# The first head of the second half of a retention and convolution decoder layer: two projection quads run in turn, both in seven block products

## The chip, the cores and the metric

The kernel runs on one core of one Trainium2 chip. The metric is the time of one execution on the device in microseconds (us), taken as the median over runs. TensorE is called PE here, VectorE DVE, ScalarE ACT, GpSimd POOL, and SyncE, whose queue issues nearly all transfers, SP.

## What is computed

```python
def mixer_layer(h, norm_g, w_in, conv_w, ret_norm_g, w_out, pos):
    hn = rms_norm(h, norm_g)
    proj = jnp.einsum('bld,de->ble', hn, w_in)                 # 1024 -> 8 * 512
    cx, cb, cc, cg, q, k, v, rg = jnp.split(proj, N_PROJ, axis=-1)
    conv_out = short_conv_branch(cx, cb, cc, conv_w) * jax.nn.silu(cg)
    qf = rotary(q.reshape(shp), pos) * (RET_HEAD_DIM ** -0.5)  # 4 heads of 128
    kf = rotary(k.reshape(shp), pos)
    ret = head_group_norm(retention_chunkwise(qf, kf, vf), ret_norm_g)
    mixed = jnp.concatenate([conv_out, ret * jax.nn.silu(rg)], axis=-1)
    return h + jnp.einsum('ble,ed->bld', mixed, w_out)
```

16 meta tokens stand ahead of a sequence of 2048, all in float32; a last RMS norm follows.

## The kernel before

The sequence is worked in two rounds (`r`) of 1024 columns, each round in two column blocks of 512 (`j`). In a round come eight units: four retention heads and four convolution groups. In round 0 the order ends with convolution group 3, and round 1 begins with head 0. Each unit needs two **quads**. A quad is a product of four weight blocks (K or Q and V or gate, against two halves of the model dimension) with the four blocks of x (two halves by two column blocks). Keys and values are the first quad of a head, queries and gates the second.

To keep the accuracy of float32, every operand is split in a high and a low part (`mh`, `ml` of x, `wh`, `wl` of a weight): ACT casts the high part, DVE subtracts it to get the low part (`split`, lines 116 to 125). A block product over four slices of 128 is three matmuls per slice, 12 in all, each 128 by 128 against 512 columns.

There are two ways to run a quad. `quad` (line 241) does it in **seven** block products, by sums of blocks in the manner of Strassen and Winograd: 84 matmuls. Its operands are x blocks 0, 1, 5 and four sums of x blocks (slots 2, 3, 4, 6 of `operand`), and seven weight blocks, which go through a ring of three buffers (`wh`, `wl`, `RING = 3`). Products 0, 2, 4 and 6 accumulate in one PSUM bank, 1 in a second, 3 and 5 in a third. After product 0, 2 and 3 ACT copies the bank (line 259), after 1, 4, 5 and 6 the `take` of the unit adds the copy on DVE and goes on. `quad_plain` (line 298) does the quad in **eight** products, from the plain blocks: 96 matmuls.

The sums of x for round 1 are made during round 0 and stored (`sums_x`). Round 1's first head uses `quad_plain` for keys and values, from 16 loads of x (`moving`) and four weights that are kept whole in operand slot 3 (`plain_parts`). Two of the four sums are loaded and split behind that, the other two by `rest_of_sums` after the first quad, together with the late gating of convolution group 3 (`gate_late`, lines 722 to 728: four DVE multiplies, two activations on ACT, two POOL multiplies). Then `quad` does queries and gates.

Keys and queries go through `rotary` (lines 738 to 745: four DVE instructions, of which the first two work on 64 partitions each). Values and keys are turned by a transposing DMA (`part`, `cross`).

Every engine runs its instructions in the order in which a list scheduler put them when the program was built; it moves instructions within what the data allow. `tc.issue_after(ins)` gives it one more rule of order. Semaphores make an engine wait for a value that another one has not yet made; what stands behind the waiting instruction on that engine waits too.

Of the kernel before, what the change touches and what calls it, by code (L numbers as in the profile page):

```python
# [8 lines left out]
F32 = mybir.dt.float32  # L9
# [69 lines left out]
def hybrid_trunk(ctx: ExitStack, tc: tile.TileContext, t, out: bass.AP, chunk_decay):  # L79
# [102 lines left out]
    def moving(load, scale=None, after={}, behind={}):  # L182
# [11 lines left out]
                    after.get((j, k), lambda: None)()  # L194
        return m, blocks

    def block_sums(b11, b12, b22, b21, t1, t3, f, g):

        def less(out, a, factor, b):
            if factor is None:
                sub(nc.vector, out, a, b)
            else:
                nc.vector.scalar_tensor_tensor(out=out, in0=a, scalar=factor, in1=b, op0=ALU.mult, op1=ALU.subtract)  # L205

        if f is not None:
# [15 lines left out]

    loaded = [None]

    def prepared(m, src, ns, held={}):

        for n in ns:
            for kt in range(KH):
                a = held.get((n, kt))  # L230
                if a is None:
                    a = gen("t")[:, :HB]
                    loaded[0] = nc.sync.dma_start(a, src[n, kt])
                parts(m, SUMS[n], kt, a)

    def idle():
# [4 lines left out]
    def quad(w, m, take, steps=()):  # L241


        steps = iter(steps)

        def product(i, bank, first):
            (wh, wl) = w[i]
            for kt in range(KH):
                ks = slice(kt * P, (kt + 1) * P)
                mh, ml = m[i][kt]  # L250
                for n, (a, b) in enumerate(((wl, mh), (wh, ml), (wh, mh))):
                    nc.tensor.matmul(  # L252
                        bank, a[:, ks], b, start=first and kt == 0 and n == 0, stop=kt == KH - 1 and n == 2,
                        skip_group_check=not first,
                    )
# [24 lines left out]
        product(4, xb, False)  # L280
        take(1, 1, xb, c)
        product(5, zb, False)
        take(0, 1, zb, u2)
        product(6, xb, False)
        take(1, 0, xb, None)

    def plain_part(n, load, slot):
        a = sb.tile([P, HB], F32, name="ra", tag="ra", bufs=RAW)
# [175 lines left out]
    def load_x(r):  # L464
        def load(k, j):
            a = gen("x")[:, :HB]
            if r == 0:
# [82 lines left out]
    def w_loads(n, r=0):  # L550
# [4 lines left out]
        return [lambda a, b=b: nc.sync.dma_start(a, b) for b in blocks]  # L555

    def kept_sums(n, r):
        return sums_a[n] if r == 0 and n in KEPT else None

    mixed = [  # L560
        dram.tile([2, 2, 2, P, KH, P], F32, name=f"mixed{b}", tag=f"mixed{b}") for b in range(SEQ // HB)
# [196 lines left out]
    def part(a, to_cross=None):  # L758
# [3 lines left out]
        if to_cross is None:  # L762
            cross(across, apart)
        else:
            to_cross.append((across, apart))
        return across

    waiting = [[], []]
# [13 lines left out]
    def head(h, r, m, rot_t, f, turning, blocks, ahead, sums, first=(), between=((), idle, idle, idle)):  # L782
# [1 line left out]

        to_cross, queried = [], []
# [5 lines left out]
        def take(i, j, pp, c):  # L793
            if i == 1 and c is None:
                v[j] = part(pp, to_cross if len(first) else None)
                return
            d = gen("kv")[:, :HB]
            if c is None:
                nc.scalar.copy(out=d, in_=pp)
            else:  # L800
                add(nc.vector, d, pp, c)
            if i == 0:
                rotary(d, tables[j])
                k[j] = d
            else:
                v[j] = d
                late.append(j)

        if len(first) > 0:
            quad_plain(first[0], m, take)  # L810
        else:
            with tc.issue_after(spreading[0].ins) if r + h == 0 else nullcontext():
                w = stationary(blocks[0], nc.vector if r + h == 0 else nc.gpsimd, kept_sums(2 * h, r))
            quad(w, m, take, between[0] or (finish_late,))
            catch_up(0)
        between[1]()
        if to_cross:
            with tc.issue_after(loaded[0].ins):
                for pair in to_cross:
                    cross(*pair)  # L820
        q, sg = [None, None], [None, None]

        def take(i, j, pp, c):
            d = gen("qg")[:, :HB]
            if i == 0:
                if c is None:
                    nc.scalar.copy(out=d, in_=pp)
                else:
                    add(nc.vector, d, pp, c)
                rotary(d, tables[j])  # L830
# [18 lines left out]
        def split_late():  # L849
            for j in late:  # L850
                v[j] = part(v[j])
            split_keys(0)

        def join(j):
# [15 lines left out]
            join_keys(0)  # L870
            between[3]()

        quad(stationary(load_raw(w_loads(2 * h + 1, r)), keep=kept_sums(2 * h + 1, r)), m, take, (split_late, middle, late_middle))
        with tc.issue_after(copied[0].ins):
            join(1)
            weigh(1)
            join_keys(1)
        between[2]()
        with tc.issue_after(queried[0].ins):
            next(sums, None)  # L880
# [191 lines left out]
    for r in range(NR):  # L1072
# [7 lines left out]
        if r == 0:  # L1080
# [70 lines left out]
                            parts(m, i, kt, held[kt])  # L1151

            between = (), idle, idle, idle
            later = prepare(load_x(1), sums_x, gain_of)
        else:
            m, b = moving(load_x(r), gain_of)
            first = [plain_parts(w_loads(0))]
            load_tables()
            prepared(m, sums_x, (1, 3))

            def rest_of_sums():
                with queued((lowered[0],)):
                    store_kept = kept.pop()()
                prepared(m, sums_x, (0, 2))
                with tc.issue_after(loaded[0].ins):
                    store_kept()

            between = (), rest_of_sums, idle, idle
# [74 lines left out]
```

## Time and profile before

| what | us |
|---|---|
| median of 3 runs | 866.44 (866.12 to 867.37) |
| the profiled execution, its own time | 865.16 |
| its span in the trace | 863.4 |
| PE busy | 854.4 (99% of the span) |
| DVE busy | 678.4 (79%) |
| ACT busy | 500.5 (58%) |
| POOL busy | 279.6 (32%) |

The page of the profile gives busy time by engine, groups of instructions by source line, and the chain of work that ended last. Durations of one instruction overlap with the next one's: what an instruction costs its engine in a row of equal ones is the distance from start to start, and it is read from rows in which several are merged. The profiled execution is 1.28 us below the median.

### The profile page before, as it was taken

The page shows a single profiled execution, that of the slowest core. Times are in us where ns is not written, and L with a number is a line of the kernel's source. Part 1 is how long each engine was busy: PE and PEld are TensorE (multiplying, and loading weights), DVE is VectorE, ACT ScalarE, POOL GpSimd, SP SyncE. Part 2 cuts the span into 40 slices and gives each one's busy share as a digit, 9 for nine tenths or more (in the row PEclk, how much of TensorE's full clock was granted, in tenths as well). Part 3 has the DMA queues.
Part 4 walks back from the last instruction along what each step waited for, and adds up shares of the span by engine and source line. Part 5 has one row for each costly group of instructions (what it writes and reads, how often), then busy time and mean ns, then how long its engine had stood idle before and what let it go on. Part 6 is the DMA issues. An engine that isn't in the chain of part 4 may idle for free.

```text
span 863.4 us, 12846 instructions
## 1 busy us (share of the span) xinstructions
PE 854.4 (99%) x4216; PEld 705.7 (82%) x4216; DVE 678.4 (79%) x1206; ACT 500.5 (58%) x901; POOL 279.6 (32%) x224
## 2 busy tenths in 40 slices
PE   9999999999999999999999999999999999999996
PEld 6778888878887778888888888888888878888885
DVE  6798989889897977979677787976655699766653
ACT  8775648474855654948284757544433575555553
POOL 0022332422245554110000002341312153777773
PEclk9999999999999999999999999999999999999999
DMA  8736257565777744966275667557344684555431
GB/s 320 244 127 167 91 147 215 146 190 184 183 232 244 244 147 159 341 195 171 74 186 170 167 189 177 174 135 256 101 118 122 201 323 147 159 177 178 147 134 74
DMA packets 141187, 154.43 MB, mean 179 GB/s; under 512 B 59904, under 2 KB 77632, under 8 KB 141120
## 3 DMA queue, kind: packets, MB, share of 16 engines
q1 hardware_dynamic: 140544, 153.21, 58.0%
q8 instruction: 33, 0.54, 0.3%
q10 hardware_dynamic: 576, 0.40, 0.2%
q14 instruction: 34, 0.28, 0.1%
HBM read 101.14 MB, written 39.85 MB: 163 GB/s over the span
## 4 chain that ended last, share of the span: by engine, by line
PE 95%; DVE 2%; DMA 1%; ACT 1%; issue 1%; POOLq 0%; SPq 0%; DVEq 0%
PE pj L252 76%; PE pj L333 5%; PE pj L309 5%; PE ms L919 2%; PE ms L908 2%; PE ms L918 2%; PE ms L895 2%; PE ms L506 1%; DMA w<-in_w_out 1%; PE ms L1057 1%; DVE wl L120 0%; DVE qg L948 0%; DVE x L205 0%; PE ms L381 0%; DVE u L663 0%
## 5 line engine op out<-in xcount | busy, mean ns | idle before, releaser
L252 PE MATMUL pj<-mh,wl 128*128 128x512 f32 x1008 | 395.8, 393 | 0.8 <-DVE wl L120 0.4
L252 PE MATMUL pj<-mh,wh 128*128 128x512 f32 x1008 | 393.2, 390 | 0.0
L252 PE MATMUL pj<-ml,wh 128*128 128x512 f32 x1008 | 392.7, 390 | 0.0
L119 ACT CAST wh<-ra 128x512 fp32r<-128x512 f32 x229 | 142.2, 621 | 253.5 <-PE pj L252 217.0
L120 DVE TENSOR_TENSOR wl<-ra,wh 128x512 fp32r<-128x512 f32 x229 | 189.1, 827 | 63.4 <-ACT wh L119 61.9
L252 PEld LDWEIGHTS pj<-mh,wl 128*128 128x128 f32 x1008 | 189.3, 188 | 41.8 <-ACT tc L259 1.2
L252 PEld LDWEIGHTS pj<-mh,wh 128*128 128x128 f32 x1008 | 189.2, 188 | 39.3
L252 PEld LDWEIGHTS pj<-ml,wh 128*128 128x128 f32 x1008 | 189.3, 188 | 38.3
L131 POOL TENSOR_TENSOR ra<-ra 128x512 f32<-128x512 f32 x44 | 67.7, 1540 | 80.6 <-PE ms L506 38.5
L931 POOL TENSOR_TENSOR rp<-rs,neg_half 128x4 f32<-128x4 f32 x16 | 19.2, 1202 | 149.8 <-DVE rs L128 149.6
L259 ACT COPY tc<-pj 128x512 f32<-128x512 f32 x108 | 62.8, 581 | 0.1
L128 POOL TENSOR_TENSOR sa<-ra 128x512 f32<-128x512 f32 x22 | 32.5, 1478 | 57.7 <-DMA ra<-in_w_in 46.6
L131 POOL TENSOR_TENSOR ra<-sa,ra 128x512 f32<-128x512 f32 x22 | 30.7, 1396 | 30.1 <-DVE wl L120 20.9
L994 DVE TENSOR_TENSOR yo<-pj,yo 128x512 f32<-128x512 f32 (+1 forms) x33 | 21.9, 672 | 23.1 <-PE pj L252 15.4
L1005 POOL TENSOR_TENSOR z<-yo,final_g 128x512 f32<-128x512 f32 x16 | 26.5, 1654 | 20.0 <-DVE yo L994 20.0
L935 DVE TENSOR_SCALAR pm<-ms,mv,rp 128x128 f32<-128x128 f32 x64 | 21.8, 403 | 11.0 <-POOL rp L931 11.0
L128 POOL TENSOR_TENSOR yo<-yo,tc 128x512 f32<-128x512 f32 x18 | 27.4, 1527 | 5.9 <-ACT tc L259 5.8
L663 POOL TENSOR_TENSOR c<-c,tc 128x512 f32<-128x512 f32 x12 | 18.6, 1551 | 31.8 <-ACT tc L693 28.4
L128 DVE TENSOR_TENSOR tc<-pj,tc 128x512 f32<-128x512 f32 x26 | 17.8, 684 | 14.1 <-PE pj L252 14.1
L663 POOL TENSOR_TENSOR c<-c,rr 128x512 f32<-128x512 f32 x12 | 18.8, 1563 | 27.1 <-DVE c L713 17.0
L581 DVE SCALAR_TENSOR_TENSOR c<-u,conv_w,c 128x512 f32<-128x512 f32 x32 | 25.2, 830 | 2.3 <-POOL u L572 1.2
L123 DVE SCALAR_TENSOR_TENSOR ml<-x,gain,mh 128x512 fp32r<-128x512 f32 x32 | 22.7, 746 | 5.1 <-ACT mh L122 5.0
(166 smaller groups left out, 1215.9 us busy)
## 6 DMA issues: line engine op xcount, KB each, us to landing
ra<-in_w_in SPq DMA_DIRECT2D x111, 256.0 KB, 2.9
ra<-sums_a SPq DMA_DIRECT2D x52, 256.0 KB, 2.9
x<-in_xT SPq DMA_DIRECT2D x48, 256.0 KB, 4.9
sums_a<-ra SPq DMA_DIRECT2D x42, 256.0 KB, 2.1
w<-in_w_out SPq DMA_DIRECT2D x32, 256.0 KB, 5.3
ra<-mixed SPq DMA_DIRECT2D x32, 256.0 KB, 2.6
yo<-in_x SPq DMA_DIRECT2D x32, 256.0 KB, 4.5
ra<-in_x SPq DMA_DIRECT2D x16, 256.0 KB, 3.3
```

The lines of the kernel that those rows point to most:

```text
L119: nc.scalar.copy(out=hi, in_=src)
L120: lowered[0] = eng.tensor_tensor(out=lo, in0=src, in1=hi.bitcast(F32), op=ALU.subtract)
L123: nc.vector.scalar_tensor_tensor(out=lo, in0=src, scalar=scale, in1=hi.bitcast(F32), op0=ALU.mult, op1=ALU.subtract)
L128: eng.tensor_tensor(out=out, in0=a, in1=b, op=ALU.add)
L131: eng.tensor_tensor(out=out, in0=a, in1=b, op=ALU.subtract)
L252: nc.tensor.matmul(bank, a[:, ks], b, start=first and kt == 0 and n == 0, stop=kt == KH - 1 and n == 2, skip_group_check=not first,)
L259: copied[0] = nc.scalar.copy(out=c, in_=bank)
L309: nc.tensor.matmul(banks[i], a[:, ks], b, start=half + kt + n == 0, stop=half == 1 and kt == KH - 1 and n == 2,)
L333: nc.tensor.matmul(banks[n][i], a[:, ks], b, start=half + kt + s == 0, stop=half == 1 and kt == KH - 1 and s == 2,)
L581: nc.vector.scalar_tensor_tensor(out=c, in0=u[:, tap : tap + HB], scalar=conv_w[:, g, tap : tap + 1], in1=c, op0=ALU.mult, op1=ALU.add)
L663: eng.tensor_tensor(out=out, in0=a, in1=b, op=ALU.mult)
L1005: nc.gpsimd.tensor_tensor(out=ys[i][j], in0=y, in1=final_g[:, j * HB : (j + 1) * HB], op=ALU.mult)
```

## The change

Round 1's first head runs both of its quads together, each in seven products. `quads` takes product 0 of keys and values, then product 0 of queries and gates, then product 1 of both, and so on to product 6; the four `pj` banks of PSUM hold both quads. I call product i of the first quad Pia and that of the second Pib. The 14 weight blocks come one by one through the same ring of three, each split right behind the products of the pair in front (`weights_in_turn`). Loads are issued in one line in the order of use: x blocks of product 0, two weights, x blocks of product 1, two weights, the sums of products 2 and 3, and so on; the second column block of the first half of x (slot 7) is not loaded any more. The late gating of convolution group 3 is put behind the splits of the last sum (`close_sums`, T4). The function `take` of a head becomes `take_keys` and `take_queries`, with one more rule of order for the first rotaries (`early`).

```diff
+    def moving_in_turn(load, scale, sums, ws):
+        m = [[] for _ in range(8)]
+        def blocks(half, j, kts=range(KH)):
+            for kt in kts:
+                k = half * KH + kt
+                parts(m, BLOCK[half][j], kt, load(k, j), scale(k) if scale else None)
+        blocks(0, 0)
+        leading = [next(a) for a in ws]
+        blocks(1, 0, range(KH // 2))
+        with tc.issue_after(copied[0].ins):
+            blocks(1, 0, range(KH // 2, KH))
+        steps = [
+            lambda: sums(m, 1), lambda: sums(m, 0), lambda: sums(m, 2), lambda: blocks(1, 1), lambda: sums(m, 3),
+        ]
+        return m, leading, steps
...
+    def quads(ws, w, m, takes, between=()):
...
+        for i in range(7):
+            for n in range(len(ws)):
+                if i < 2:
+                    banks[n][i] = ps_proj()
+                product(n, i, banks[n][i in (1, 3, 5)], i in (0, 1, 3))
+            w = [next(a, None) for a in ws]
+            for n, take in enumerate(takes):
+                bank = banks[n][i in (1, 3, 5)]
+                if i == 0:
+                    copies[n] = copy(bank)
+                elif i == 1:
+                    take(0, 0, bank, copies[n])
...
+                else:
+                    take(1, 0, bank, None)
+            next(between, idle)()
...
+    def weights_in_turn(n, r):
+        for load in w_loads(n, r, in_line):
+            a = raw()
+            load(a)
+            yield weight_parts(a)
...
             if i == 0:
-                rotary(d, tables[j])
+                with queued(early if j == 0 and len(first) else ()):
+                    rotary(d, tables[j])
                 k[j] = d
...
-        if len(first) > 0:
-            quad_plain(first[0], m, take)
...
+        if len(first) > 0:
+            steps = list(first[1:4]) + [lambda: (first[4](), split_keys(0)), idle, split_values, lambda: split_keys(1)]
+            quads(*first[0], m, (take_keys, take_queries), steps)
+            join_keys(0)
+            join(1)
+            weigh(1)
+            join(0)
+            weigh(0)
             join_keys(1)
...
-            m, b = moving(load_x(r), gain_of)
-            first = [plain_parts(w_loads(0))]
+            ws = [weights_in_turn(n, r) for n in range(2)]
+            m, leading, first = moving_in_turn(
+                load_x(r), gain_of, lambda m, n: prepared(m, sums_x, (n,), in_turn=True), ws
+            )
             load_tables()
-            prepared(m, sums_x, (1, 3))
-
-            def rest_of_sums():
-                with queued((lowered[0],)):
+
+            def open_sums(t2=first[0], t1=first[1]):
+                t2()
+                t1()
+                early.append(lowered[0])
+
+            def close_sums(t4=first[4]):
+                t4()
+                with tc.issue_after(lowered[0].ins):
                     store_kept = kept.pop()()
-                prepared(m, sums_x, (0, 2))
                 with tc.issue_after(loaded[0].ins):
                     store_kept()
```

The built order shows where instructions stand. On PE, at the end of convolution group 3 (line 252, `quad`) the order before has 25 matmuls of the head's plain quad (line 309) ahead of the group's product 5, whose x operand is mh_275:

```order
L309 MATMUL pj<-mh_3907,mh_3973 128x512
L309 MATMUL pj<-mh_3907,ml_3974 128x512
L309 MATMUL pj<-ml_3908,mh_3973 128x512
L252 MATMUL pj<-mh_275,wl 128x512
L252 MATMUL pj<-ml_276,wh 128x512
L252 MATMUL pj<-mh_275,wh 128x512
```

In the changed order the group's last product (x operand mh_461; `quad` is at line 274 now) is followed by the head's P0a (line 322, `quads`), and all 168 matmuls of the two quads stand in one piece behind it:

```order
L274 MATMUL pj<-mh_461,wl 128x512
L274 MATMUL pj<-ml_462,wh 128x512
L274 MATMUL pj<-mh_461,wh 128x512
L322 MATMUL pj<-mh_3865,wl 128x512
L322 MATMUL pj<-ml_3866,wh 128x512
L322 MATMUL pj<-mh_3865,wh 128x512
```

The 25 matmuls no longer stand between the group's products 4 and 5.

On DVE, in the quad of queries and gates, the order before has the weight split of product 3 (`wl<-ra,wh`, the second of these rows that has a weight) ahead of the add of product 1 (`qg<-pj,tc`, line 128) and of the rotary that follows it (lines 742 to 745); mh_4188 to mh_4207 are operands of product 4:

```order
L120 TENSOR_TENSOR ml_4189<-t,mh_4188 128x512
L120 TENSOR_TENSOR wl<-ra,wh 128x512
L120 TENSOR_TENSOR ml_4195<-t,mh_4194 128x512
L128 TENSOR_TENSOR qg<-pj,tc 128x512
L120 TENSOR_TENSOR ml_4201<-t,mh_4200 128x512
L120 TENSOR_TENSOR ml_4207<-t,mh_4206 128x512
L742 TENSOR_TENSOR rot<-qg,rot_t 64x512
L743 TENSOR_TENSOR rot<-qg,rot_t 64x512
L120 TENSOR_TENSOR wl<-ra,wh 128x512
L744 TENSOR_TENSOR qg<-qg,rot_t 128x512
```

In the changed order the rows from the add of P1b to the weight splits of P3a and P3b (`x2`) are these (rotary is lines 817 to 820 now, mh_4070 to mh_4088 are product 4's operands):

```order
L128 TENSOR_TENSOR qg<-pj,tc 128x512
L819 TENSOR_TENSOR kv<-kv,rot_t 128x512
L820 TENSOR_TENSOR kv<-kv,rot 128x512
L817 TENSOR_TENSOR rot<-qg,rot_t 64x512
L818 TENSOR_TENSOR rot<-qg,rot_t 64x512
L120 TENSOR_TENSOR ml_4071<-t,mh_4070 128x512
L120 TENSOR_TENSOR ml_4077<-t,mh_4076 128x512
L819 TENSOR_TENSOR qg<-qg,rot_t 128x512
L120 TENSOR_TENSOR ml_4083<-t,mh_4082 128x512
L120 TENSOR_TENSOR ml_4089<-t,mh_4088 128x512
L820 TENSOR_TENSOR qg<-qg,rot 128x512
L120 TENSOR_TENSOR wl<-ra,wh 128x512 x2
```

Eleven DVE instructions now stand from the add of P1b up to the weight split of P3a, and that split stands behind the rotaries instead of ahead of them.

Further on in DVE's changed order come the operands of products 5 and 6, and then the late gating (line 738) ahead of the weight split of P5a, which is the last row here:

```order
L120 TENSOR_TENSOR wl<-ra,wh 128x512 x2
L120 TENSOR_TENSOR ml_4199<-t,mh_4198 128x512
L120 TENSOR_TENSOR ml_4205<-t,mh_4204 128x512
L120 TENSOR_TENSOR ml_4211<-t,mh_4210 128x512
L120 TENSOR_TENSOR ml_4217<-t,mh_4216 128x512
L738 TENSOR_TENSOR cg<-cg,rr 128x512
L738 TENSOR_TENSOR c<-c,rr 128x512
L738 TENSOR_TENSOR cg<-cg,rr 128x512
L738 TENSOR_TENSOR c<-c,rr 128x512
L120 TENSOR_TENSOR wl<-ra,wh 128x512
```

In the order before, the four gating multiplies stood among the splits of x, before the second half of the plain quad's matmuls.

## Rows read from the trace of the kernel before

**Rows 1.** The page, parts 1 and 2: PE busy, and its granted clock in tenths.
```profile
PE 854.4 (99%) x4216; PEld 705.7 (82%) x4216; DVE 678.4 (79%) x1206; ACT 500.5 (58%) x901; POOL 279.6 (32%) x224
...
PEclk9999999999999999999999999999999999999999
```
**Rows 2.** The chain that ended last, in order of time: start us, us, what.
```profile
0.99 4.45 PE ms L1057 x10
...
353.70 5.44 PE pj L252 x24
359.14 5.67 PE pj L309 x25
364.81 5.44 PE pj L252 x24
370.25 16.09 PE pj L309 x71
386.34 19.04 PE pj L252 x84
...
406.27 5.46 PE pj L252 x24
```
**Rows 3.** The longest waits of PE for another engine: us in total, times, longest.
```profile
PE ms L1057 <- DVE warm L1049: 1.0, 1, 1.0
PE pj L252 <- DVE wl L120: 0.4, 1, 0.4
```
**Rows 4.** ACT in order of time, end of convolution group 3.
```profile
354.96 0.58 ACT L259 COPY tc<-pj 128x512 f32<-128x512 f32 x1
...
360.32 0.59 ACT L259 COPY tc<-pj 128x512 f32<-128x512 f32 x1
```
**Rows 5.** Transfers from 340 to 430 us: KB each, median us from issue to landing.
```profile
x<-in_xT SPq DMA_DIRECT2D x16, 256.0 KB, 5.6
```
**Rows 6.** SP in order of time: the 16 loads of x.
```profile
347.12 9.06 SPq L470 DMA_DIRECT2D x<-in_xT  x16
```
**Rows 7.** DVE in order of time: splits, rotaries, and an add behind a product.
```profile
352.99 2.73 DVE L123 SCALAR_TENSOR_TENSOR ml<-x,gain,mh 128x512 fp32r<-128x512 f32 x4
...
365.89 2.49 DVE L120 TENSOR_TENSOR ml<-t,mh 128x512 fp32r<-128x512 f32 x4
...
387.79 0.69 DVE L744 TENSOR_TENSOR kv<-kv,rot_t 128x512 f32<-128x512 f32 x1
...
389.13 1.28 DVE L120 TENSOR_TENSOR ml<-t,mh 128x512 fp32r<-128x512 f32 x2
...
395.86 0.69 DVE L742 TENSOR_TENSOR rot<-qg,rot_t 64x512 f32<-64x512 f32 x1
396.56 0.69 DVE L743 TENSOR_TENSOR rot<-qg,rot_t 64x512 f32<-64x512 f32 x1
397.28 0.69 DVE L120 TENSOR_TENSOR wl<-ra,wh 128x512 fp32r<-128x512 f32 x1
...
411.83 0.69 DVE L128 TENSOR_TENSOR kv<-pj,tc 128x512 f32<-128x512 f32 x1 [1.44 <-PE pj L252]
```
**Rows 8.** POOL in order of time: two stretches with DVE at work.
```profile
334.75 1.30 POOL L131 TENSOR_TENSOR ra<-ra 128x512 f32<-128x512 f32 x1
...
380.51 3.45 POOL L663 TENSOR_TENSOR c<-c,cg 128x512 f32<-128x512 f32 x2 [32.13 <-ACT cg L725]
```
**Rows 9.** DVE in the same two stretches.
```profile
334.94 1.66 DVE L120 TENSOR_TENSOR wl<-ra,wh 128x512 fp32r<-128x512 f32 x1 [1.42 <-ACT wh L119]
...
380.88 0.68 DVE L745 TENSOR_TENSOR kv<-kv,rot 128x512 f32<-128x512 f32 x1
```
**Rows 10.** Stretches at the end: busy us of PE, PEld, DVE, ACT, POOL; PEclk; DMA, GB/s.
```profile
855.00:856.50 1.50, 1.23 (x6) 0.68 (x4) 0.55 (x3) 0.39 (x2) 0.55 (x1) 1.00 0.00 0
...
858.00:859.50 1.50, 0.00 (x0) 0.00 (x0) 0.74 (x3) 0.57 (x1) 0.55 (x1) 1.00 0.76 283
859.50:861.00 1.50, 0.00 (x0) 0.00 (x0) 0.18 (x1) 0.15 (x1) 0.00 (x0) 0.62 0.34 128
```

More of the change, by code (lines that the diff above doesn't have):

```diff
@@ L224, in hybrid_trunk, with prepared @@
     loaded = [None]
-    def prepared(m, src, ns, held={}):
+    def prepared(m, src, ns, held={}, in_turn=False):
         for n in ns:
@@ L232, in prepared @@
                     a = gen("t")[:, :HB]
-                    loaded[0] = nc.sync.dma_start(a, src[n, kt])
+                    if in_turn:
+                        in_line(a, src[n, kt])
+                    loaded[0] = line[0] if in_turn else nc.sync.dma_start(a, src[n, kt])
                 parts(m, SUMS[n], kt, a)
@@ L285, in quad, with product, copy @@
         take(1, 0, xb, None)
+    def quads(ws, w, m, takes, between=()):
+        between = iter(between)
+        banks = [[None, None] for _ in ws]
+        copies = [None for _ in ws]
+        def product(n, i, bank, first):
+            wh, wl = w[n]
+            for kt in range(KH):
+                ks = slice(kt * P, (kt + 1) * P)
+                mh, ml = m[i][kt]
+                for s, (a, b) in enumerate(((wl, mh), (wh, ml), (wh, mh))):
+                    nc.tensor.matmul(
+                        bank, a[:, ks], b, start=first and kt == 0 and s == 0, stop=kt == KH - 1 and s == 2,
+                        skip_group_check=not first,
+                    )
+        def copy(bank):
+            c = sb.tile([P, HB], F32, name="tc", tag="tc", bufs=COPIES)
+            copied[0] = nc.scalar.copy(out=c, in_=bank)
+            return c
+        for i in range(7):
[10 more added lines that the diff above has]
+                    take(0, 0, bank, copies[n])
+                elif i == 2:
+                    copies[n] = [copy(bank)]
+                elif i == 3:
+                    copies[n].append(copy(bank))
+                elif i == 4:
+                    take(1, 1, bank, copies[n][1])
+                elif i == 5:
+                    take(0, 1, bank, copies[n][0])
+                else:
+                    take(1, 0, bank, None)
+            next(between, idle)()
     def plain_part(n, load, slot):
@@ L462, in in_line, with load_x @@
             line[0] = nc.sync.dma_start(out, src)
-    def load_x(r):
+    def load_x(r, first=True):
         def load(k, j):
             a = gen("x")[:, :HB]
-            if r == 0:
+            if first:
                 in_line(a, t["xT"][r, j, k])
@@ L548, in hybrid_trunk, with w_loads @@
     KEPT = [n for n in range(4 * NG) if n // 2 != NG]
-    def w_loads(n, r=0):
+    def w_loads(n, r=0, load=nc.sync.dma_start):
         if r and n in KEPT:
@@ L554, in w_loads @@
             blocks = [t["w_in"][n, i] for i in range(4)]
-        return [lambda a, b=b: nc.sync.dma_start(a, b) for b in blocks]
+        return [lambda a, b=b: load(a, b) for b in blocks]
     def kept_sums(n, r):
         return sums_a[n] if r == 0 and n in KEPT else None
+    def weights_in_turn(n, r):
[3 more added lines that the diff above has]
+            yield weight_parts(a)
     mixed = [
@@ L756, in cross, with part @@
         )
-    def part(a, to_cross=None):
+    def part(a):
         apart, across = gen("pl")[:, :HB], gen("tr")[:, :HB]
         nc.scalar.copy(out=planes(apart), in_=halves(a))
[L762 to L765, printed above, removed]
+        cross(across, apart)
         return across
-    waiting = [[], []]
+    waiting, early = [[], []], []
     def catch_up(stage):
@@ L791, in head, with take_keys @@
         tables = [rot_t[:, :, j * HB : (j + 1) * HB] for j in range(2)]
-        def take(i, j, pp, c):
+        def take_keys(i, j, pp, c):
             if i == 1 and c is None:
-                v[j] = part(pp, to_cross if len(first) else None)
+                v[j] = part(pp)
                 return
@@ L807, in take, with take_queries @@
                 late.append(j)
-        if len(first) > 0:
-            quad_plain(first[0], m, take)
[L811 to L820, printed above, removed]
         q, sg = [None, None], [None, None]
-        def take(i, j, pp, c):
+        def take_queries(i, j, pp, c):
             d = gen("qg")[:, :HB]
@@ L829, in take @@
                     add(nc.vector, d, pp, c)
-                rotary(d, tables[j])
+                with queued(early if j == 0 and len(first) else ()):
+                    rotary(d, tables[j])
                 queried.append(turned[0])
@@ L847, in join_keys, with split_values, split_late @@
             nc.scalar.copy(out=halves(kt[j]), in_=planes(across_k[j]))
-        def split_late():
+        def split_values():
             for j in late:
                 v[j] = part(v[j])
+        def split_late():
+            split_values()
             split_keys(0)
@@ L871, in late_middle @@
             between[3]()
-        quad(stationary(load_raw(w_loads(2 * h + 1, r)), keep=kept_sums(2 * h + 1, r)), m, take, (split_late, middle, late_middle))
-        with tc.issue_after(copied[0].ins):
+        if len(first) > 0:
+            steps = list(first[1:4]) + [lambda: (first[4](), split_keys(0)), idle, split_values, lambda: split_keys(1)]
+            quads(*first[0], m, (take_keys, take_queries), steps)
+            join_keys(0)
             join(1)
             weigh(1)
+            join(0)
+            weigh(0)
             join_keys(1)
+        else:
+            with tc.issue_after(spreading[0].ins) if r + h == 0 else nullcontext():
+                w = stationary(blocks[0], nc.vector if r + h == 0 else nc.gpsimd, kept_sums(2 * h, r))
+            quad(w, m, take_keys, between[0] or (finish_late,))
+            catch_up(0)
+            between[1]()
+            w = stationary(load_raw(w_loads(2 * h + 1, r)), keep=kept_sums(2 * h + 1, r))
+            quad(w, m, take_queries, (split_late, middle, late_middle))
+            with tc.issue_after(copied[0].ins):
+                join(1)
+                weigh(1)
+                join_keys(1)
         between[2]()
@@ L1153, in hybrid_trunk @@
             between = (), idle, idle, idle
-            later = prepare(load_x(1), sums_x, gain_of)
+            later = prepare(load_x(1, False), sums_x, gain_of)
         else:
-            m, b = moving(load_x(r), gain_of)
-            first = [plain_parts(w_loads(0))]
+            ws = [weights_in_turn(n, r) for n in range(2)]
+            m, leading, first = moving_in_turn(
+                load_x(r), gain_of, lambda m, n: prepared(m, sums_x, (n,), in_turn=True), ws
+            )
             load_tables()
-            prepared(m, sums_x, (1, 3))
-            def rest_of_sums():
-                with queued((lowered[0],)):
+            def open_sums(t2=first[0], t1=first[1]):
[5 more added lines that the diff above has]
+                with tc.issue_after(lowered[0].ins):
                     store_kept = kept.pop()()
-                prepared(m, sums_x, (0, 2))
                 with tc.issue_after(loaded[0].ins):
                     store_kept()
-            between = (), rest_of_sums, idle, idle
+            first = [(ws, leading), open_sums, first[2], first[3], close_sums]
+            between = (), idle, idle, idle
             blocks = None, None
```

2 lines of the change are left out of this document (1 added, 1 removed).

## The prediction

> **What bounds the kernel now.** I read the page first. PE is busy for 99% of the span at its full granted clock [rows 1]. Then the chain that ended last: through the stretch that the change touches it never leaves PE [rows 2]. Then PE's waits: after the start it waits for another engine 0.4 us at most [rows 3]. So a matmul taken away here is worth its own spacing, and a wait added here costs its full length, as nothing else is late. What decides is whether DVE and ACT, which follow the data in a fixed order, still have each operand ready.
>
> The spacing: 24 matmuls take 5.44 us [rows 2], 0.2267 us each, so a block product of 12 takes 2.72 us.
>
> **What the change removes.** The head had 25 + 71 plain matmuls and 84 of the seven-product quad [rows 2], 180 together. It has 2 x 84 = 168 now. Twelve at 0.2267 us: **-2.72 us**, all on PE's path.
> The Trainium skill, "TensorE: Matmul & The Clock Gate", section "Wait — 56ns, not 53.3ns?", puts such a matmul at 215.7 ns, by which the gain would be an estimated 2.59 us; the rows here say 226.7 ns, and I go by them.
>
> **What cover goes at the end of convolution group 3.** Before, 25 matmuls of the head stood ahead of the group's product 5, 5.67 us of them [rows 2]. Product 5 needs ACT's copy of product 3's bank, which came only at 360.32 [rows 4]. Without the cover, product 5 starts at 353.70 + 5.44 = 359.14 on the chain, some 0.16 us earlier by its first matmul, say 358.98. Between the two copies [rows 4] ACT had nine instructions, and the second copy is the tenth: 5.36 us / 10 = 0.54 us a step. In the changed order there are five between: 354.96 + 6 x 0.54 = 358.2 us, and with its 0.59 us the copy ends at 358.8 [rows 4]. One x cast less stands ahead of the first copy as well, so the margin is 0.2 to 0.8 us. I put it at nothing; each tenth by which ACT is later than that would cost a tenth.
>
> **Loads.** Four x loads go, three weight loads come, and the order is that of use. The 16 loads of x were issued from 347.12 in 9.06 us and landed 5.6 us after issue [rows 5, 6], so sixteen were in by about 362 us: 0.75 us each from 350. At that rate the 28th load in line, the last weight of product 3, is in by 371 us, and the 42nd by 382 us. P3a is due at 380.7 us and P6a at 397 us (next part). Nothing, then: transfers are 10 us ahead.
>
> **The wait that the change adds.** With no wait PE would go through: group 3's four products end at 353.70 + 4 x 2.72 = 364.58 us, the first four of the pair (P0a, P0b, P1a, P1b) at 375.46, P2a and P2b at 380.90, and P3a's first matmul would start 0.16 us ahead of that, at 380.74.
> P3a needs its weight split. In DVE's order that split stands behind the add of P1b, which can't start before P1b is done: such an add starts at 411.83 in the trace, 0.10 us behind a product that ended at 406.27 + 5.46 = 411.73 [rows 2, 7], so here at 375.56. From there, from start to start, each with its row [rows 7]:
> - the add of P1b, at the distance of equal instructions, (2.49 - 0.69) / 3 = 0.60;
> - the last two steps of the keys' rotary (744, 745), one behind the other, 389.13 - 387.79 = 1.34;
> - the first two steps of the queries' rotary (742, 743), 397.28 - 395.86 = 1.42;
> - two low parts of product 4, the third rotary step, two low parts, the fourth rotary step: 6 x 0.60 = 3.60;
> - P3a's weight split itself, 0.69.
>
> Sum 7.65 us: the split ends at 383.21. PE starts up to 0.1 us later, at 383.3, against 380.74: **+2.55 us**. The order before had the split of product 3 ahead of add and rotary; here PE has only P2a and P2b, 5.44 us, to cover 7.65. Behind the waiting matmul stands all of PE's queue, so the wait goes to the end in full.
> Bounds: if all twelve went at 0.60, 11 x 0.60 + 0.69 = 7.29, a wait of 2.1 us; if each took its whole 0.69, 8.28, a wait of 3.2 us with a late start. I take 2.55, as each step has its own row. ACT is not the one that is late: behind P2a's end (378.2) come its copy and two casts of product 4 and that of P3a's weight, at 0.6 us each, as the copies take [rows 4], so the first cast is done by 379.5, and DVE comes to its low part at 375.56 + 0.60 + 1.34 + 1.42 + 3 x 0.60 = 380.7.
>
> **The late gating** (four DVE multiplies, two activations, two POOL multiplies) moves to just ahead of P5a's weight split. From P3a's split (start 382.52) DVE has two weight splits, four x low parts ((2.73 - 0.69) / 3 = 0.68 each [rows 7]), two weights, four sums, four gating multiplies and P5a's split: 2 x 0.60 + 4 x 0.68 + 10 x 0.60 + 0.69 = 10.6, so 393.1 us, 0.3 us later if it waits for a cast. P5a is due at 383.3 + 4 x 2.72 = 394.2: a margin of about 0.9 us. But the two POOL multiplies, 3.45 us together [rows 8], now run beside these DVE instructions. In one stretch a POOL instruction stretched a DVE split from 0.69 to 1.66 us, in another DVE kept its 0.68 [rows 8, 9]. So 0 to 2 x 0.97 us on DVE, and 0 to 1.0 us on PE behind the margin. I take **+0.1 us**, nearer to nothing: both hits must fall ahead of the split.
>
> Three more adds on DVE, one split less, and the copies of both quads lie beside matmuls and end no wait. Keys and values are turned later against the head's end, but the next head's products 0 to 3 (4 x 2.72 us) are put ahead of the retention matmuls, which cover that.
>
> **Sum:** -2.72 + 2.55 + 0.1 = -0.07 us. Against the profiled execution's 865.16 us that is 865.1; its own time lies 1.28 us below the median, so on the median 866.44 - 0.07 = **866.4 us**: no change. The gain is there, and a new wait of the same length eats it.
>
> **Rivals.**
> *The wait isn't there, or is short: faster.* If DVE reached P3a's split within 5.44 us, the 2.72 us would be left, 863.7 us, with a wait of 1 us 864.7. For it: no wait of PE of that kind is in the trace before. Against it: DVE's order is fixed, eleven instructions stand there, and even at the shortest distances they take 7.29 us.
> *The clock falls: slower.* Before, PE never idled for more than half a us between start and end, so the trace doesn't show what its clock does after an idle 2.55 us in mid-run. The ten warm-up matmuls at the start took 4.45 us [rows 2], where ten at full rate take 2.27. If the wait dropped the array to its lower level (1.2 GHz) for such a stretch, it would cost about 2.2 us more: 866.4 + 2.2 = 868.6 us. It decides if the granted clock behind the wait is under 1.00. Against it: at the end PE stops at 856.2, and the granted clock is still 1.00 (2.4 GHz) in the stretch up to 859.5, 3.3 us later, and lower only after [rows 10].
> The Trainium skill, "TensorE: Matmul & The Clock Gate", section "What's actually happening", holds that the throttled state is the default and that activity releases it; by that an idle PE may lose its clock. The trace agrees as far as the end shows it.
> *ACT or POOL add more: slower, but little.* With the whole 1.0 us of the gating and a wait of 3.2 us the sum is +1.5 us, 867.9.
>
> **How the numbers follow.** About 0.2% (1.7 us) is what a measurement here can tell from no change. The forecast, with waits of 2.1 to 3.2 us and gating of 0 to 1.0 us, runs from 866.44 - 0.6 = 865.8 to 867.9, all within 0.2%; chance 0.80, a small part of which falls out at either side by the scatter of the medians (866.12 to 867.37 before). The faster case, 863.7 to 864.7: 0.09. The clock's: 0.06. Several small waits together over 1.7 us: 0.05. So faster 0.09, within 0.2% 0.80, slower 0.11. The range takes in the forecast with its bounds, the scatter, and the faster case's upper end: 864.7 to 868.2 us.
>
> **What would show it.** In the changed profile PE has one new wait of about 2.5 us ahead of a product of the head, at about 381 to 383 us, ended by a weight split of DVE (line 120), with DVE busy without a gap for the 7.6 us before it. PE has 12 matmuls fewer. The head's 168 matmuls take 168 x 0.2267 = 38.1 us plus that wait. The granted clock stays 1.00. I am wrong if that wait is under 1 us (then faster), if a second wait of over 1 us follows, at P5a or in the group before, or if matmuls behind the wait are spaced at 0.43 us instead of 0.23.

## The result and the profile after

| | median us | ratio to before |
|---|---|---|
| before, 20 runs | 866.06 | |
| the changed kernel, 20 runs | 867.62 | 1.0017 (95%: 1.0011 to 1.0024) |

So the change costs 1.5 us, 0.17% of the time. One of the changed kernel's 20 runs, at 899 us, was a slow one and is left out of the ratio. The forecast was no change, 866.4 us. The time lies in the range given (864.7 to 868.2), but a loss was measured where none was forecast, and it is clear of the scatter.

The profiled execution doesn't explain it. Its own time is 866.15 us (span 864.4). The page, part 1, as in [rows 1]:

```profile
PE 851.4 (99%) x4204; PEld 702.9 (81%) x4204; DVE 687.6 (80%) x1208; ACT 498.5 (58%) x901; POOL 282.0 (33%) x224
```

Twelve matmuls are gone. The page's row of the clock reads 9 throughout, as before. That settles little: each of its slices is 21.6 us long and 9 stands for 90% or more, so a few us at half the clock don't show in it (a later profile below, in which the clock falls, has the same row). Short stretches would show a fall. Here are two behind the new wait (busy us of PE, PEld, DVE, ACT, POOL; granted clock; DMA, GB/s), at the full clock:

```profile
383.00:386.00 3.00, 2.06 (x9) 1.69 (x10) 3.00 (x6) 3.00 (x6) 0.00 (x0) 1.00 0.01 1
386.00:389.00 3.00, 3.00 (x15) 2.48 (x14) 2.69 (x5) 2.46 (x5) 0.00 (x0) 1.00 1.00 248
```

The waits of PE for another engine (total, times, longest), to be held against [rows 3]:

```profile
PE pj L322 <- DVE wl L120: 2.5, 1, 2.5
PE pj L274 <- DVE wl L120: 1.4, 1, 1.4
PE ms L1138 <- DVE warm L1130: 1.0, 1, 1.0
PE pj L274 <- ACT tc L281: 0.2, 1, 0.2
```

The first is the forecast one, ahead of P3a. The second stands at 296 us in round 0, where the programs are the same; it was 0.4 us in [rows 3] and 1.4 us when the kernel before was profiled again, so it belongs to the single execution. That second profile of before has this row:

```profile
PE pj L252 <- DVE wl L120: 1.4, 1, 1.4
```

The last, at 411 us, is new at that place. DVE in order of time, from the add of P1b to the weight split of P3a, and the weight split of P5a:

```profile
376.11 0.69 DVE L128 TENSOR_TENSOR qg<-pj,tc 128x512 f32<-128x512 f32 x1
376.72 0.68 DVE L819 TENSOR_TENSOR kv<-kv,rot_t 128x512 f32<-128x512 f32 x1
...
382.60 0.69 DVE L820 TENSOR_TENSOR qg<-qg,rot 128x512 f32<-128x512 f32 x1
383.20 1.29 DVE L120 TENSOR_TENSOR wl<-ra,wh 128x512 fp32r<-128x512 f32 x2
...
393.52 0.69 DVE L120 TENSOR_TENSOR wl<-ra,wh 128x512 fp32r<-128x512 f32 x1
```

The chain that ended last (start us, us, what), from P3a on:

```profile
383.21 0.69 DVE wl L120
...
383.94 19.39 PE pj L322 x84
...
404.39 4.93 DMA tr<-pl
...
409.35 0.04 ACT v L921
...
410.57 0.41 ACT wh L119
...
411.08 0.59 ACT tc L281
...
411.72 5.75 PE pj L274 x24
```

Behind the head the chain leaves PE: ACT's joining copy of the values (line 921) waits for the transposing DMA, which lands 4.93 us after its issue, and ahead of the next head's copy (line 281) ACT must finish it. That is the 0.2 us. By the list of waits the change is worth -2.72 + 2.50 + 0.24 = +0.02 us. But the list counts idle time alone. PE in order of time shows more:

```profile
381.05 0.39 PE L322 MATMUL pj<-mh,wh 128*128 128x512 f32 x1
383.94 0.50 PE L322 MATMUL pj<-mh,wl 128*128 128x512 f32 x1 [2.50 <-DVE wl L120]
384.28 0.40 PE L322 MATMUL pj<-ml,wh 128*128 128x512 f32 x1
...
411.09 0.39 PE L274 MATMUL pj<-mh,wh 128*128 128x512 f32 x1
411.72 0.50 PE L274 MATMUL pj<-mh,wl 128*128 128x512 f32 x1 [0.24 <-ACT tc L281]
412.06 0.39 PE L274 MATMUL pj<-ml,wh 128*128 128x512 f32 x1
```

From start to start, less the usual spacing of 0.23 us, the two waits cost 2.66 and 0.40 us, and the step behind each takes 0.34 us in place of 0.23. That makes -2.72 + 2.77 + 0.51 = +0.56 us. The same matmuls held side by side in the two traces agree: from 347 us in the trace before, ahead of the head, to 465 us, behind it, the changed kernel falls back by about 0.7 us. So the profile bears out the sum to some 0.7 us. The median lies 1.5 us above before, so something happens in other executions that this one doesn't show.

The list of executions gave the hint. Each has the mean granted clock of TensorE over its span. Of the 19 that the comparison uses, 11 have 0.995 or 0.996 and a median of 868.06 us; 8 have 0.997 or 0.998, among them the profiled one, and a median of 866.11 us. The second group agrees with before to 0.05 us. The mean is rounded to 0.001, so it doesn't sort every execution; the kernel before, run beside the experiments, has 0.997 to 0.999.

### The profile page after: what moved, and what is told of

Its sections match the earlier page's. It is cut to its first block, busy times and chain, and to the rows that moved or that the text cites. A ratio compares the mean times of both kernels' runs of the same rounds, so it can differ in the third digit from the quotient of the medians.

```text
span 864.4 us, 12823 instructions
## 1 busy us (share of the span) xinstructions
PE 851.4 (99%) x4204; PEld 702.9 (81%) x4204; DVE 687.6 (80%) x1208; ACT 498.5 (58%) x901; POOL 282.0 (33%) x224
## 4 chain that ended last, share of the span: by engine, by line
PE 52%; DMA 1%; ACT 1%; issue 1%; DVE 1%; SPq 0%; POOLq 0%; ACTq 0%; DVEq 0%
PE pj L274 44%; PE pj L378 2%; PE pj L322 2%; PE ms L1000 1%; PE ms L989 1%; PE ms L999 1%; PE ms L976 1%; DMA w<-in_w_out 1%; DMA tr<-pl 1%; ACT mh L119 0%; ACT wh L119 0%; ACT tc L281 0%; DVE yo L1110 0%; DVE wl L120 0%; SPq L546 0%
## 5 line engine op out<-in xcount | busy, mean ns | idle before, releaser
L274 PE MATMUL pj<-mh,wl 128*128 128x512 f32 x980 | 384.9, 393 | 1.7 <-DVE wl L120 1.4
L274 PE MATMUL pj<-mh,wh 128*128 128x512 f32 x980 | 382.3, 390 | 0.0
L274 PE MATMUL pj<-ml,wh 128*128 128x512 f32 x980 | 381.8, 390 | 0.0
L119 ACT CAST wh<-ra 128x512 fp32r<-128x512 f32 x236 | 146.4, 621 | 246.1 <-PE pj L274 202.7
L120 DVE TENSOR_TENSOR wl<-ra,wh 128x512 fp32r<-128x512 f32 x236 | 197.2, 839 | 60.3 <-ACT wh L119 57.7
L274 PEld LDWEIGHTS pj<-mh,wl 128*128 128x128 f32 x980 | 184.1, 188 | 41.6 <-ACT tc L281 3.2
L274 PEld LDWEIGHTS pj<-mh,wh 128*128 128x128 f32 x980 | 184.0, 188 | 38.3
L274 PEld LDWEIGHTS pj<-ml,wh 128*128 128x128 f32 x980 | 184.1, 188 | 37.2
L281 ACT COPY tc<-pj 128x512 f32<-128x512 f32 x105 | 60.9, 580 | 0.1
L1110 DVE SCALAR_TENSOR_TENSOR yo<-yo,rf,final_g 128x512 f32<-128x512 f32 x16 | 17.6, 1100 | 11.0 <-POOL rf L417 11.0
```

The source lines that it names most:

```text
L119: nc.scalar.copy(out=hi, in_=src)
L120: lowered[0] = eng.tensor_tensor(out=lo, in0=src, in1=hi.bitcast(F32), op=ALU.subtract)
L274: nc.tensor.matmul(bank, a[:, ks], b, start=first and kt == 0 and n == 0, stop=kt == KH - 1 and n == 2, skip_group_check=not first,)
```

## The experiments

Three theories went to the chip. **Clock:** in most executions the granted clock falls behind the pause ahead of P3a. **Transposes:** the wait near 411 us is usually far longer than in the profile. **Round 0:** the wait at 296 us is what varies.

**The two kernels once more.**

> The changed kernel once more, unchanged, for a second profile and more times. Three theories for the 1.5 us that the medians lie above before, though the profiled execution shows the forecast waits and no more. Clock theory: in most executions the granted clock falls for some 3.5 us behind the 2.5 us pause of PE; among the 20 executions the mean granted clock is 0.995 to 0.996 where the span is 865.6 us or more and 0.997 to 0.998 where it is 865.4 or less, and the profiled one was of the second kind. It expects the same split here, and, if the profiled execution is of the longer kind, matmuls at double spacing behind the wait at about 384 us. Transpose theory: the wait of PE near 411 us on ACT's copy, 0.24 us in the first profile, is 1.5 to 2 us in most executions, and the clock has nothing to do with it. Round-0 theory: the wait at about 296 us (0.45 us before, 1.39 us in the profile after, where the program is the same) is what varies. Time expected by all: 867.6 us.

> The kernel before as a kernel of its own: a measure of what no change reads as. All theories: ratio 1.000, within 0.1%; 866.1 us. The clock theory expects a mean granted clock of 0.998 in nearly all executions, since PE never pauses for over half a us there. The round-0 theory expects spans to scatter here as much as after the change.

> The changed kernel unchanged, on the chip of the three kernels beside it, as their base. Clock theory: nearly all executions at a mean granted clock of 0.995 to 0.997 and near 868 to 869 us, as in the run before, where six of seven executions stood so; if the profiled execution is of that kind, the granted clock is under 1.00 for some 3.5 us behind the wait at about 384 us and the matmuls there stand 0.43 us apart. Rival, that the extra time comes from waits in the data (transposes, ACT): the profile, if it is of the longer kind, shows a longer wait and the granted clock stays 1.00.

Before against itself: ratio 1.0003 (0.9994 to 1.0011), 865.88 us. The changed kernel: 868.89 us on the one chip, where six of seven executions stood at 868.6 to 869.2 (two of them with a mean clock of 0.997, where the clock theory had expected 0.995 or 0.996) and only the profiled one at 866.34; 868.72 us on another, where the profiled one took 869.37 us with a mean clock of 0.996. That profile shows what happens. Stretches of it (busy us of PE, PEld, DVE, ACT, POOL; PEclk; DMA, GB/s):

```profile
380.00:382.50 2.50, 2.50 (x12) 1.75 (x10) 2.47 (x5) 1.99 (x4) 0.00 (x0) 1.00 0.00 0
382.50:385.00 2.50, 0.02 (x1) 0.00 (x0) 2.50 (x6) 2.44 (x5) 0.00 (x0) 1.00 0.01 3
385.00:386.50 1.50, 1.47 (x6) 1.23 (x7) 1.50 (x3) 1.50 (x3) 0.00 (x0) 0.99 0.00 0
386.50:389.90 3.40, 3.40 (x9) 2.67 (x8) 2.33 (x4) 1.62 (x4) 0.00 (x0) 0.50 0.83 201
389.90:393.00 3.10, 3.10 (x15) 2.56 (x14) 2.68 (x5) 3.10 (x8) 0.00 (x0) 1.00 0.88 276
```

PE in order of time, same execution:

```profile
385.03 0.50 PE L322 MATMUL pj<-mh,wl 128*128 128x512 f32 x1 [2.50 <-DVE wl L120]
...
386.55 0.63 PE L322 MATMUL pj<-mh,wl 128*128 128x512 f32 x1
386.98 0.63 PE L322 MATMUL pj<-ml,wh 128*128 128x512 f32 x1
...
389.94 0.39 PE L322 MATMUL pj<-mh,wh 128*128 128x512 f32 x1
390.16 0.39 PE L322 MATMUL pj<-mh,wl 128*128 128x512 f32 x1
```

The wait is the same 2.50 us. PE resumes at 385.03 at full rate, and at 386.5 the granted clock falls to 0.50, 1.2 GHz, for 3.4 us: matmuls stand 0.43 us apart. The fourteen from 385.03 to 389.94 take 4.91 us, where 14 x 0.2267 = 3.17 do at full rate: 1.74 us lost. In the two profiles without the fall the same fourteen take 3.32 and 3.35 us, as the first steps behind the wait are slower there too, so 1.6 us is the clock's own. The waits on ACT's copies in this profile are 0.6 us at the longest, and that one stands in round 0; behind the head it is 0.2 us, so the transposes theory does not give the difference. The wait at 296 us reads 1.4 us as in the first profile, so neither does the third. Held side by side with the profile at 866.34 us, this one falls back by 1.0 us ahead of the head, by 1.7 us in it, and by 0.4 us behind it.

**The pause filled.** Matmuls on the zero tile of the warm-up go into the pause; no other engine waits for them. A rule of order, not shown, keeps the later products behind them.

```diff
+            if i == 2:
+                with tc.issue_after(last[0].ins):
+                    filled[0] = warm_up(10)    # 4 in the second kernel
             w = [next(a, None) for a in ws]
...
```

> The changed kernel with ten matmuls on the zero tile of the warm-up put on PE just ahead of product 3 of keys and values, 10 x 0.2267 = 2.27 us in the pause of 2.5 us; nothing waits for them and nothing else moves. Clock theory: the wait on DVE's weight split falls to 0.2 us, its end doesn't move, the granted clock stays, and the median falls by 1.5 us or more to about 866.0 us, mean clock 0.998 in nearly all executions. Transpose theory and round-0 theory: the product can't start earlier, so the time stays at 867.6 us.

> The changed kernel with four matmuls on the zero tile at the start of the pause in place of ten, 4 x 0.2267 = 0.9 us, so that PE pauses for about 1.6 us in place of 2.5. The product that waits can't start earlier either way. Clock theory: what the clock costs shrinks or goes: a median between that of the changed kernel and 2.3 us less (the fall with ten). Rival, no clock: the median of the changed kernel.

With ten: 866.57 us, ratio to before 1.0007 (0.9998 to 1.0016), 2.3 us less than the changed kernel on the same chip. With four: 866.11 us, ratio 1.0005 (0.9996 to 1.0014), 2.6 us less. All 22 executions have a mean clock of 0.997 or more, and none took more than 867.6 us. The waits for DVE, first with ten and then with four:

```profile
PE pj L325 <- DVE wl L120: 0.3, 1, 0.3
```
```profile
PE pj L325 <- DVE wl L120: 1.6, 1, 1.6
```

And the stretches of the kernel with four:

```profile
382.00:383.50 1.50, 0.09 (x1) 0.09 (x1) 1.50 (x4) 1.50 (x4) 0.00 (x0) 1.00 0.02 5
383.50:386.50 3.00, 3.00 (x13) 2.46 (x14) 3.00 (x5) 2.48 (x5) 0.00 (x0) 1.00 0.39 72
386.50:390.00 3.50, 3.50 (x17) 2.90 (x16) 3.19 (x7) 3.50 (x7) 0.00 (x0) 1.00 0.87 279
```

P3a doesn't start earlier in either kernel: from the start of the add of P1b to its first matmul pass 7.82 and 7.83 us, and 383.94 - 376.11 = 7.83 in the changed kernel. So work that computes nothing buys 2.3 to 2.6 us. A part of that is not the clock's: in both profiles the joining copy at the end of the head doesn't wait for the transposing DMA, which is worth up to 0.5 us. Of the three theories only the clock's allows the rest. A pause of 1.6 us with 0.9 us of work ahead of it left no sign of a lower clock in 11 executions: they took 865.1 to 867.2 us, and before took 864.6 to 867.3 on that chip.

**The pause made longer.** Five DVE copies of a tile onto itself ahead of P3a's weight split:

```diff
+            with tc.issue_after(slow[0].ins) if i == 2 else nullcontext():
+                w = [next(a, None) for a in ws]
...
+                if len(first) and j == 0:
+                    for _ in range(5):
+                        slow[0] = nc.vector.tensor_copy(out=d, in_=d)
                 queried.append(turned[0])
...
```

> The changed kernel with five copies of a 128x512 tile onto itself on DVE between the first rotary of the queries and the weight split of product 3, so that the pause is longer by 5 x 0.33 to 5 x 0.6, 1.7 to 3 us. Clock theory: the clock falls in every execution, so that the profiled one too shows a granted clock under 1.00 and matmuls 0.43 us apart behind the pause; median 1.7 to 3 us above the changed kernel's on the same chip. Rival, no clock: the same rise, and the granted clock 1.00 in every stretch behind the pause.

873.67 us. The pause grew to 7.0 us, by 4.5 and not by 1.7 to 3: besides the copies, at 0.33 us each, DVE now has four low parts of x (line 123, 0.67 us each) ahead of the split, which stand behind it in the changed kernel. I hadn't counted them. All five executions have a mean clock of 0.992 to 0.994, as the clock theory expected. The stretches:

```profile
379.00:381.60 2.60, 2.60 (x12) 1.88 (x10) 2.55 (x5) 2.12 (x4) 0.00 (x0) 1.00 0.02 6
381.60:383.90 2.30, 0.06 (x1) 0.00 (x0) 2.30 (x5) 2.21 (x4) 0.00 (x0) 0.99 0.01 4
383.90:388.60 4.70, 0.00 (x0) 0.00 (x0) 4.67 (x11) 4.70 (x9) 0.00 (x0) 0.50 0.52 109
388.60:394.00 5.40, 5.35 (x13) 4.19 (x14) 5.40 (x10) 0.82 (x2) 0.44 (x1) 0.50 0.48 148
394.00:397.00 3.00, 3.00 (x15) 2.48 (x14) 2.07 (x3) 2.78 (x4) 2.84 (x2) 0.99 0.09 28
```

The clock is at half from 383.9, while PE still stands, until 394: 5.4 us of PE's work at half rate, 2.7 us lost. Sum -2.72 + 7.0 + 2.7 = +7.0 us; measured against before on that chip, 873.67 - 866.27 = +7.4.

**A pause in the kernel before, and the same pause filled.** No seven-product pair here, no change of loads: a matmul between products 3 and 4 of queries and gates waits for POOL; the second kernel has fourteen matmuls on the zero tile ahead of it.

```diff
         c = copy(zb)
+        if pause:
+            src = c[:, :P]
+            for _ in range(3):
+                nc.gpsimd.tensor_copy(out=src, in_=src)
+            with tc.issue_after(last[0].ins):
+                full = warm_up(14)    # only in the second kernel
+            bank = ps_misc()
+            with tc.issue_after(full.ins):    # last[0] in the first
+                paused[0] = nc.tensor.matmul(bank[:, :P], src, src, start=True, stop=True)
```

> The kernel before, with a pause of PE and nothing else, in the quad of queries and gates of round 1's first head: a matmul between products 3 and 4 that waits for three copies of 128 columns on POOL, which wait for ACT's copy of product 3. The pause x is read from the profile, an estimate of 1.5 to 2.5 us (0.6 for ACT, its wait ahead, and three short POOL instructions). Clock theory: if the pause is as long as the one of the change, the median rises by x and 1.5 to 2.5 us more, and the mean granted clock falls by 0.002 against before's 0.997 to 0.999. Rival, that the extra time of the change comes from waits elsewhere: the median rises by x and no more, and the clock stays.

> The kernel before with the same wait on POOL as in the run with the pause, and fourteen matmuls on the zero tile ahead of it, 14 x 0.2267 = 3.17 us, so that PE works through nearly all of the 3.4 us that it paused there. The path of the wait is unchanged. Clock theory: the granted clock stays 1.00, and of the 6.7 us that the pause cost, 3.4 to 3.6 us are left: about 869.8 us. Rival, that the extra 3.3 us come from the waits or from the changed order behind them: the time stays at about 872.9 us.

872.93 us paused, 871.04 us filled. Stretches of the paused one:

```profile
395.00:397.80 2.80, 2.79 (x13) 1.98 (x11) 2.75 (x5) 2.80 (x6) 0.00 (x0) 1.00 0.75 129
397.80:400.00 2.20, 0.00 (x0) 0.00 (x0) 2.03 (x5) 2.20 (x6) 0.20 (x1) 1.00 1.02 371
400.00:401.20 1.20, 0.00 (x0) 0.00 (x0) 0.67 (x1) 1.20 (x5) 1.05 (x3) 0.50 1.01 235
401.20:406.80 5.60, 5.57 (x14) 4.50 (x15) 0.00 (x0) 2.28 (x2) 0.00 (x0) 0.50 0.46 114
406.80:410.00 3.20, 3.20 (x17) 2.67 (x17) 2.06 (x4) 0.79 (x2) 0.00 (x0) 1.00 0.17 27
```

Products 4 and 5 in the chain, paused and filled:

```profile
402.03 7.76 PE pj L254 x24
```
```profile
402.15 5.49 PE pj L254 x24
```

They start at the same place, as the path through POOL is the same; the paused kernel's take 2.27 us longer. The medians differ by 1.89, and by 1.4 when each is taken against the runs of before beside it (6.66 and 5.23 us above). So the clock's price arises in the kernel before as well, without the change. The pause itself was longer than the 1.5 to 2.5 us expected: from the end of product 3 (397.8) to product 4 (402.03) it is 4.2 us, and 4.2 + 2.27 = 6.5 us is nearly all of the 6.66. All five paused executions have a mean clock of 0.994 to 0.996. My 869.8 for the filled one was too low: I had taken the 3.4 us of the wait list, but to its product 4 (402.15) it is 4.3 us; some 0.9 us beyond that I can't assign.

**The wait taken away.** The loads and splits of the sum for product 4 (T3) go one step earlier, so that DVE comes to P3a's weight split before the queries' rotary.

```diff
-            first = [(ws, leading), open_sums, first[2], first[3], close_sums]
+            def open_three(t3=first[2]):
+                open_sums()
+                t3()
+            first = [(ws, leading), open_three, idle, first[3], close_sums]
```

> The changed kernel with the loads and splits of the sum for product 4 (T3) one step earlier, ahead of product 1, so that DVE has the weight split of product 3 ahead of the rotaries, as before the change. All theories: the 2.5 us wait ahead of product 3 goes. Transpose theory and round-0 theory: the median falls by just 2.5 us, to about 865.1 us, and what makes the median longer than the profile stays. Clock theory: the pause is gone and with it the lower clock, so the median falls by 2.5 + 1.5 = 4 us, to about 863.6 us, less what the later transposes cost near 408 us, 0.1 to 0.4 us.

> The version with T3 one step earlier once more, for its time against before. Clock theory: 12 matmuls less (2.72 us), no pause, no fall of the clock, and 0.4 us of wait on ACT's copy near 409 us: before's median less 2.3 us, ratio 0.9973, and every execution at a mean granted clock of 0.997 to 0.999. Rival, that it was chance: ratio 0.999 to 1.000.

863.91 and 863.86 us, ratios 0.9976 (0.9967 to 0.9985) and 0.9976 (0.9966 to 0.9985): this version beats both kernels, by 1.9 us and, on the same chip, by 5.0 us. The fall of 5.0 is twice the wait that was removed. Held side by side with the first profile of the change, where the clock didn't fall, both profiles gain 2.8 us up to the end of the head; the other 2.1 us or so fit the price of the clock. P3a's weight split on DVE, and then PE, which runs through; no execution has a mean clock under 0.997:

```profile
377.47 0.68 DVE L120 TENSOR_TENSOR wl<-ra,wh 128x512 fp32r<-128x512 f32 x1
```

```profile
380.00:383.00 3.00, 3.00 (x15) 2.47 (x14) 2.95 (x6) 3.00 (x6) 0.00 (x0) 1.00 0.00 0
383.00:386.00 3.00, 3.00 (x15) 2.48 (x14) 3.00 (x6) 3.00 (x7) 0.00 (x0) 1.00 0.86 190
```

Of the 2.72 us of fewer matmuls the wait on ACT's copy behind the transposes takes back 0.4 to 0.7 us in the two profiles, from start to start less one spacing; that is what is left of the transposes theory.

## Why the prediction was wrong

Its sum was right to some 0.7 us; the step that failed is the argument against its own clock rival, by which the fall of the clock stood in the sum at nothing.

- **Twelve matmuls, -2.72 us:** right.
- **End of group 3, nothing:** right. ACT's second copy there starts at 357.70 (forecast 358.2), and PE doesn't wait:

```profile
357.70 0.59 ACT L281 COPY tc<-pj 128x512 f32<-128x512 f32 x1
```

- **Loads, nothing:** right, no wait of PE for a transfer of the head.
- **The wait ahead of P3a, +2.55 us:** right, 2.50 us in all three profiles that follow this order; with the slower first steps of PE behind it, it costs 2.8 us. From the add of P1b to the end of the split DVE took 383.89 - 376.11 = 7.78 us against 7.65. One reading behind it was off: in the order rows of before, the weight split ahead of the add is product 4's, and the later one product 5's. Product 3's stands still further ahead of that add, which starts at 393.95, so the argument holds:

```profile
390.33 0.68 DVE L120 TENSOR_TENSOR wl<-ra,wh 128x512 fp32r<-128x512 f32 x1
```

- **The late gating, +0.1 us:** nothing. P5a's weight split ended at 394.21, and P5a's first matmul started at 395.00. Beside POOL's multiplies (392.54 to 397.06) a DVE split took 1.18 us in place of 0.69, but it was P5b's, which had the time.
- **"The next head's products 0 to 3 cover that":** not quite. ACT runs in order, and the values' join stands ahead of the copy for product 1. By the list PE waits 0.24 us here; from start to start, with the slower step behind it, 0.4 to 0.5 us in all three profiles of the changed kernel. A small miss.
- **The clock, chance 0.06:** this decided. I held against it that at the end of the run the clock was still 1.00 over 3 us after PE had stopped [rows 10]. That was one stop in one execution, and I read it as if the clock always outlasts a pause of 2.5 us. In the runs it was at half 2.2 us after PE stopped (400.0 against 397.8) in one kernel, 2.3 us in another (383.9 against 381.6), and in the changed kernel 4.0 us after, when PE was already at work again. The condition that I gave, a granted clock under 1.00 behind the wait, was seen in one of three profiles, with the matmuls 0.43 us apart that I had named as a sign of being wrong; by the mean clock it holds in about 11 of 19 executions. The price that I gave, 2.2 us from the warm-up, measured 1.6 to 1.7 in that profile, and 1.95 between the medians of the two groups. With 11 of 19 executions in the longer group the median of all falls among the lower ones of that group, 867.6 us.

An estimate of the shares: 11 of 19 times 1.6 us is 0.9 us. The mean of the 19 executions lies 1.55 us above that of before (867.37 against 865.82), and the 0.6 us left are near the +0.56 us that the profile shows without the clock. That the time fell into the range I gave is luck: the range reached up to 868.2 for other reasons than the clock. And the 0.2% that I took as the least that can be told from no change was too wide; the interval here is 0.11% to 0.24%.

The sentence on which I had weighed the rule of the Trainium skill, "TensorE: Matmul & The Clock Gate", section "What's actually happening", that activity releases the throttle, ended with the trace agreeing "as far as the end shows it". The runs here speak for the rule: behind a pause of 2.5 us the array lost its clock in about 11 of 19 executions, behind pauses of 4.2 and 7.0 us in all five each, and where matmuls that compute nothing filled the pause of 2.5 us, it showed no loss in 22.

## What to carry to other kernels

Where PE is busy throughout, a new pause like this one of 2.5 us has two prices: its length, and the clock that may fall behind it, here 1.6 to 2.0 us more in some executions and none in others; behind the pauses of 4.2 and 7.0 us it was 2.3 and 2.7 us. So the trade of twelve matmuls against a wait of equal length lost 1.5 us here. Look at the mean granted clock and the time of every execution before trusting the one that was profiled, and at the clock in stretches of a few us, as the page's row doesn't show a fall this short; and first try to bring the late operand earlier, then to fill the pause.

## What the runs showed that was not expected

- The same 2.50 us pause at the same place left the clock at 1.00 in two profiled executions and was followed by 3.4 us at half in a third; the fall came 1.5 us after PE had resumed.
- With four matmuls on a zero tile in the pause, 0.9 us of work, none of 11 executions showed a lower clock, though PE still stood for 1.6 us.
- The fall also comes with PE standing (383.9 in the kernel with the long pause), and PE then starts at half rate and works so for 5.4 us before the clock is back.
